# A hybrid attention, Fourier and Hyena layer on one core: merge gates and branch products computed token-major, their sum transposed on TensorE, and the adaLN gate summed and broadcast by one all-ones matrix

## The chip, the cores and the metric

One core of a Trainium2 chip runs the kernel. The metric is the device time of one execution in microseconds. The kernel before took 1326.72 us, the median of three runs (1324.34 to 1326.83). PE is the matrix engine TensorE, PEld its weight loads, DVE the vector engine, ACT the scalar engine, POOL GpSimd, and SP the engine that issues most DMAs here.

## The reference

One layer over 128 context and 256 latent tokens of 2048 channels, all in fp32. Cut to what this change touches:

```
proj, gate = _modulated_proj(y, c_ctx, norm_g, w_ada, b_ada, w_in)   # gate = last third of silu(c) @ w_ada + b_ada
y_a = att * silu(...)      # 1024 channels: neighbourhood attention, 8 heads
y_b = fourier * silu(...)  # 512 channels
y_c = hyena * silu(...)    # 512 channels
g_a, g_b, g_c = split(sigmoid(proj[..., OFF_MG:]), 3)      # 3 x 2048 channels
merged = g_a * (y_a @ w_br[:1024]) + g_b * (y_b @ w_br[1024:1536]) + g_c * (y_c @ w_br[1536:])
return x + gate[:, None, :] * (merged @ w_out)
```

The adaLN gate has one row of 2048 numbers for the context tokens and one for the latent tokens.

## The kernel before

**Products with the weights.** PE multiplies in fp32r. Each operand is split into a hi part (a cast) and a lo part (the rest), and a product is hi x hi + lo x hi + hi x lo: three matmuls. `products` (line 478) walks over pairs of k tiles: for each it loads a weight tile `w` of 2 x 128 rows and 512 columns (512 KB), lets ACT cast it to `wh` (line 473) and DVE subtract to `wl` (line 475), and issues first all matmuls with `wh`, then those with `wl`. There are 4 buffers of `w`, 2 of `wh`, 2 of `wl`, 5 PSUM banks `acc` for sums and 3 banks `aux` for everything else.

**Two layouts.** `chan_block` (line 504) makes a product channel-major, [channel, token]: the weights are the stationary side, 128 columns at a time, and 384 tokens stream; a pair of k tiles is 4 sums x 2 k tiles x 3 = 24 matmuls of 384 columns. `tok_block` (line 511) makes it token-major, [token, channel]: 128 tokens are stationary and 512 columns of the weights stream; a pair is 3 x 2 x 3 = 18 matmuls of 512 columns. The stationary side has the contracted channels on the partitions, so what enters a product (`h`, the branch outputs `y`, the merged sum `m`) must lie channel-major.

**The stages.** `main` (line 971) runs the Hyena input, then the Fourier and attention inputs, then, from line 987 on, the merge: for each of four blocks of 512 columns and each branch, a gate product of 8 pairs (sigmoid by ACT, line 994) and a branch product of 2, 2 or 4 pairs; DVE multiplies both (lines 999 and 1002) and POOL adds up (line 1003). The sum `merged` is channel-major. At the end it is split into `m` (line 1006). The output projection (line 1010) is token-major; DVE multiplies by the gate and adds x.

**The adaLN gate.** `ada_gate` (line 901) runs beside the merge stage. For each of four column blocks DVE multiplies 16 tiles of `w_ada` with the condition and adds them up into `part` (line 931), once for each of two rows; two fp32 matmuls by a matrix of ones with 32 columns (line 937) sum over the partitions into 32 rows, the bias is added, and at the end all is split. In the output stage `bcast_row` (line 294) picks one row and broadcasts it to 128 partitions by two fp32r matmuls for each row, four for each column block.

**The order.** `Weave` (line 130) writes the order of PE and SP in the program by a plan: each flow yields steps with a tensor time, a latency and events, and flows of lower number go first. The gate's flow is paced by 2.7 k tiles of the main flow for each of its 64 tiles (line 923). The order of ACT, DVE and POOL comes from the scheduler of the framework, by priority.

Of the kernel before, what the change touches and what calls it, by code (L numbers as in the profile page):

```python
# [10 lines left out]
F32 = mybir.dt.float32  # L11
# [7 lines left out]
P = 128  # L19
D = 2048  # L20
# [27 lines left out]
# (stream index, first token column, number of tokens, first 128-token tile, tiles)  # L48
# [6 lines left out]
def shape_constants():  # L55
    """Arrays that depend on the shapes alone."""
# [48 lines left out]
# blocks of adaLN columns: first column, columns, pace; and the sums of the Hyena input: block, pairs of k tiles  # L105
# [7 lines left out]
def small_arrays(a, consts):  # L113
    """Small arrays side by side: vectors with 128 channels on the partitions, one column each, and the identity;
    the positional features with the first two filter layers."""
    rows = [a["c"], a["c_ctx"], a["norm_g"], a["b_ada"][:, :2 * D], a["conv_w"], a["conv_b"], a["hy_bias"]]
    rows = np.concatenate([np.asarray(r).reshape(-1, P) for r in rows])
    half = np.concatenate([np.asarray(a[k]) for k in ("f_b1", "f_freq", "f_b2")])
    half = np.concatenate([half, half], axis=1)
    mlp = np.zeros((64, TOK + 192), np.float32)  # L120
    mlp[:33, :TOK] = consts.pop("zfeat")
    mlp[:33, TOK:TOK + 64] = np.asarray(a["f_w1"])[0]
    mlp[:, TOK + 64:] = np.concatenate([np.asarray(a["f_w2"])[0]] * 2, axis=1)
    a["f_w3"] = np.concatenate([np.asarray(a["f_w3"])[0]] * 2)
    a["mlp"] = mlp
    a["first"] = np.concatenate([np.concatenate([rows, half]).T, consts.pop("ident")], axis=1)
    a.update(consts)


class Weave:  # L130
    """Orders the steps of several flows for the in-order queues of TensorE and of the weight loads.

    A flow is a generator. Before each step it yields what the step asks for: the tensor time it holds, the time
    of its load, the latency after the flow's previous step, and events that come first. A flow of lower number
    goes first when its step is ready; the others fill in.
    """
# [77 lines left out]
def hybrid_block(ctx: ExitStack, tc: tile.TileContext, a: dict):  # L214
# [79 lines left out]
    def bcast_row(out, row, hi, lo):  # L294
        """One row of hi + lo to all partitions."""
        pick = ident_r[:, row:row + 1].broadcast_to([P, P])
        mm(out, pick, hi, True, False)
        mm(out, pick, lo, False, True)
# [28 lines left out]
    def rsqrt(out, ss, n, scale):  # L327
        """out = 1 / sqrt(ss * scale + EPS), all [P, n]."""
# [33 lines left out]
    def x_norm():  # L362
        """x channel-major as it comes, and 1 / rms of its tokens on all partitions."""
# [33 lines left out]
    def ada(b, c0, wd, pace, rate):  # L397
        """Columns c0 .. c0 + wd - 1 of shift and scale; then that part of h, hi and lo."""
# [66 lines left out]
    ahead = []  # L465

    def weights(src, kp, c0):
        """hi and lo parts of two k tiles of 512 columns, in two steps."""
# [9 lines left out]
    def products(src, c0, kps, n, product, evac, done=lambda kp: (), final=False):  # L478
        """n sums of the products of hi and lo parts, of two k tiles at a time: the ones with wh first, as wl comes
        later. A final block ends sum by sum, so that the evacuations spread out."""  # L480
# [23 lines left out]
    def chan_block(src, c0, kps, x, evac, done=lambda kp: ()):  # L504
        """Columns c0..c0+511, channel-major [channel, token]."""
# [4 lines left out]
    def tok_block(src, c0, x, evac, final=False):  # L510
        """Columns c0..c0+511, token-major [token, channel]."""
        def product(ps, t, kt, px, w, start, stop):
            mm(ps, x[px][kt // 4][:, kt % 4, P * t:P * t + P], w, start, stop)
        yield from products(src, c0, range(KT // 2), NT, product, evac, final=final)

# [1 line left out]
    # Even and odd tokens apart: E and O hold (real, imaginary, real with the top bin's row) of the filter's even and  # L517
    # odd part over bins 0..127; the top bin sits in row 0 of the imaginary products. C is the context's filter.
# [3 lines left out]
    def sin_layer(ps, n, col, name):  # L522
        """n rows of sin(freq * (ps + bias))."""
# [13 lines left out]
    def filters():  # L537
# [5 lines left out]
        def split_w3(x):  # L543
            """hi part on partitions 0..63, lo part on the others."""
# [110 lines left out]
    def long_conv(pool, o, z, xg):  # L655
        """z <- xg * (conv(z, filter o) + bias * z), channel-major, in place."""
# [53 lines left out]
    def fourier(u, gate):  # L710
        """Real part of the 2-D DFT of u, times the gate path (in place), channel-major."""
# [62 lines left out]
    def flip(x):  # L774
        """Latent tokens with the columns of each grid row in reverse."""
# [90 lines left out]
    # ================= the program =================  # L866
# [31 lines left out]
    # adaLN gate: rows 32 j hold columns 512 j .. 512 j + 511  # L898
    gate_rows = []

    def ada_gate():
# [4 lines left out]
        gate_b = pool.tile([P, 512], F32, name="gate_b")  # L906
        for j in range(4):
            nc.gpsimd.dma_start(out=gate_b[32 * j:32 * j + 32, :],
                                in_=b_ada[0, 2 * D + 512 * j:2 * D + 512 * j + 512].partition_broadcast(32))
        grow = [pool.tile([P, 512], F32, name=f"grow{s}") for s in range(2)]  # L910

        def load(i):
            w = pool.tile([P, 512], F32, tag="w_gate", name="w_gate", bufs=6)
# [5 lines left out]
        for j in range(4):  # L919
            part = [pool.tile([P, 512], F32, tag=f"part{s}", name=f"gate_part{s}", bufs=1) for s in range(2)]  # L920
            for kt in range(KT):
# [4 lines left out]
                for s in range(2):  # L926
                    cs = cond[:, kt, s:s + 1]
                    if kt == 0:
                        nc.vector.tensor_scalar(out=part[s], in0=w, scalar1=cs, scalar2=None, op0=ALU.mult)
                    else:  # L930
                        nc.vector.scalar_tensor_tensor(out=part[s], in0=w, scalar=cs, in1=part[s],  # L931
                                                       op0=ALU.mult, op1=ALU.add)
            yield step(0.5, lat=5.0)
            rows = slice(32 * j, 32 * j + 32)
            for s in range(2):
                pg = aux()
                mm(pg[rows, :], ones, part[s])
                nc.vector.tensor_tensor(out=grow[s][rows, :], in0=pg[rows, :], in1=gate_b[rows, :], op=ALU.add)
        for s in range(2):
            gate_rows.append(split(grow[s], pool.tile([P, 512], F32R, name=f"grow_hi{s}"),  # L940
                                   pool.tile([P, 512], F32R, name=f"grow_lo{s}")))
# [29 lines left out]
    def main():  # L971
# [15 lines left out]
        merged = []  # L987
        for ob in range(4):
            m32 = s6([P, 4, TOK], F32, f"merged{ob}")
            for bi, (br, kps) in enumerate(((2, (6, 7)), (1, (4, 5)), (0, (0, 1, 2, 3)))):  # L990
                g = s6([P, 4, TOK], F32, "mgate")

                def ev_gate(j, ps):
                    nc.scalar.activation(g[:, j, :], ps, AF.Sigmoid)
                yield from chan_block(w_in, OFF_MG + D * br + 512 * ob, range(8), h, ev_gate)

                def ev_br(j, ps):
                    if bi == 0:
                        nc.vector.tensor_tensor(out=m32[:, j, :], in0=ps, in1=g[:, j, :], op=ALU.mult)
                    else:  # L1000
                        t = tmp("mt")
                        nc.vector.tensor_tensor(out=t[:, 0:TOK], in0=ps, in1=g[:, j, :], op=ALU.mult)
                        nc.gpsimd.tensor_tensor(out=m32[:, j, :], in0=m32[:, j, :], in1=t[:, 0:TOK], op=ALU.add)  # L1003
                yield from chan_block(w_br, 512 * ob, kps, y, ev_br, lambda kp: (Y_READY[kp // 2],))
            merged.append(m32)
        m = list(zip(*[split_big(merged[ob], f"m{ob}") for ob in range(4)]))

# [1 line left out]
        osrc = [a["y_prompt"][0], a["y_sample"][0, 0:P, :], a["y_sample"][0, P:2 * P, :]]  # L1009
        for ob in range(4):  # L1010
            cs = slice(512 * ob, 512 * ob + 512)
            gts = []
            for s in range(2):
                yield step(MM2, after=("gate",), wait=4.0)
                pg = aux()
                bcast_row(pg, 32 * ob, *gate_rows[s])
                gt = s6([P, 512], F32, "gt")
                nc.scalar.copy(out=gt, in_=pg)
                gts.append(gt)

            def ev_out(t, ps):
# [3 lines left out]
                nc.vector.tensor_tensor(out=o, in0=ps, in1=gts[CONTEXT if t == 0 else LATENT], op=ALU.mult)  # L1025
# [3 lines left out]
            yield from tok_block(w_out, 512 * ob, m, ev_out, final=(ob == 3))  # L1029
# [42 lines left out]
```

## Time and profile before

| | us |
|---|---|
| median of three runs | 1326.72 |
| span of the profiled execution, all that the page gives of its time | 1331.5 |
| PE busy | 1296.1 (97%) |
| weight loads busy | 1172.4 (88%) |
| DVE busy | 712.7 (54%) |
| ACT busy | 456.6 (34%) |
| POOL busy | 191.4 (14%) |
| merge stage, from the first sigmoid to the end of the last branch product | 669.5 to about 1190 |
| output stage, its matmuls | 1190.9 to about 1324.5 |

The span is the time from the first to the last instruction in one execution. Matmuls follow each other before their results are out, so one is shown as busy for longer than the time to the next one's start; what counts on PE is the time from start to start. A line number is that of a helper where one is called: all matmuls stand at line 253, so the tiles tell them apart.

### The profile page before, as it was taken

What the parts mean: (1) busy time and instruction counts of PE and PEld (TensorE: products, weight loads), DVE (VectorE), ACT (ScalarE), POOL (GpSimd) and SP (SyncE); (2) the same over time, 40 slices, a digit from 0 to 9 for tenths busy, and PEclk for the clock granted to TensorE, in tenths of its full rate; (3) what the DMA queues carried; (4) which work ended last, traced back from release to release, by engine and by line L of the source; (5) the groups of instructions that cost most, each with busy time, mean ns of one, the idle gap of its engine ahead of it and who ended that gap; (6) DMA issues with size and microseconds to landing.
All of it is one profiled execution on the core that took longest, in us unless ns stands there. A gap on an engine that the chain in (4) does not pass through costs nothing.

```text
span 1331.5 us, 18263 instructions
## 1 busy us (share of the span) xinstructions
PE 1296.1 (97%) x7290; PEld 1172.4 (88%) x7290; DVE 712.7 (54%) x1076; ACT 456.6 (34%) x715; POOL 191.4 (14%) x211
## 2 busy tenths in 40 slices
PE   6889999999999999999999999999999999999997
PEld 4667879878888988889999999999999999998886
DVE  6567638868444335552354763754746733354442
ACT  4523324421343244433444222222222222242221
POOL 2046200135010002200110110011001100120000
PEclk9889999999999999999999999999999999999999
DMA  8888874322374446554453655554655544445551
GB/s 271 260 298 283 264 248 122 111 78 82 103 162 132 143 119 123 118 134 127 108 109 115 211 175 156 174 175 134 193 182 164 174 134 124 126 131 183 172 173 57
DMA packets 111189, 211.30 MB, mean 159 GB/s; under 512 B 8128, under 2 KB 16704, under 8 KB 111104
## 3 DMA queue, kind: packets, MB, share of 16 engines
q1 hardware_dynamic: 107200, 198.98, 48.0%
q0 software_dynamic: 3760, 11.01, 5.0%
q8 instruction: 57, 0.93, 0.3%
q14 instruction: 28, 0.23, 0.0%
q10 hardware_dynamic: 144, 0.14, 0.0%
HBM read 205.91 MB, written 4.19 MB: 158 GB/s over the span
## 4 chain that ended last, share of the span: by engine, by line
PE 91%; DMA 4%; DVE 2%; ACT 1%; POOL 1%; issue 0%; SPq 0%; ACTq 0%
PE acc L253 83%; PE aux L253 6%; DMA w<-in_w_in 3%; DVE wl L475 1%; DMA w_ada<-in_w_ada 1%; DMA x<-in_x_prompt 1%; ACT wh L473 1%; PE aux L851 0%; PE aux L783 0%; POOL yim L678 0%; DVE hc L634 0%; PE acc L376 0%; PE aux L663 0%; POOL yre L678 0%; DVE h_lo L455 0%
## 5 line engine op out<-in xcount | busy, mean ns | idle before, releaser
L475 DVE TENSOR_TENSOR wl<-w,wh 128x1024 fp32r<-128x1024 f32 x272 | 351.1, 1291 | 445.9 <-PE acc L253 308.7
L473 ACT CAST wh<-w 128x1024 fp32r<-128x1024 f32 x272 | 286.3, 1053 | 720.8 <-PE acc L253 635.5
L253 PE MATMUL acc<-h_hi,wh 128*128 128x384 f32 x1216 | 414.7, 341 | 7.7 <-DVE hc L634 2.8
L253 PE MATMUL acc<-h_lo,wh 128*128 128x384 f32 x1216 | 408.9, 336 | 0.0
L253 PEld LDWEIGHTS acc<-h_hi,wh 128*128 128x128 f32 x1216 | 230.0, 189 | 20.8 <-issue 11.1
L253 PE MATMUL acc<-h_hi,wl 128*128 128x384 f32 x1216 | 241.6, 337 | 0.0
L253 PEld LDWEIGHTS acc<-h_lo,wh 128*128 128x128 f32 x1216 | 230.0, 189 | 2.1 <-issue 0.7
L253 PEld LDWEIGHTS acc<-h_hi,wl 128*128 128x128 f32 x1216 | 212.2, 188 | 5.1 <-issue 4.4
L253 PE MATMUL acc<-wh,h_hi 128*128 128x512 f32 x336 | 135.6, 404 | 0.0
L253 PE MATMUL acc<-wh,h_lo 128*128 128x512 f32 x336 | 131.8, 392 | 0.0
L1003 POOL TENSOR_TENSOR merged<-merged,mt 128x384 f32<-128x384 f32 x32 | 40.7, 1302 | 426.8 <-ACT wh L473 240.6
L931 DVE SCALAR_TENSOR_TENSOR gate_part<-w_gate,cond,gate_part 128x512 f32<-128x512 f32 x120 | 88.0, 784 | 25.5 <-DMA w_gate<-in_w_ada 25.5
L253 PE MATMUL acc<-wl,h_hi 128*128 128x512 f32 x336 | 90.9, 400 | 0.0
L253 PEld LDWEIGHTS acc<-wh,h_hi 128*128 128x128 f32 x336 | 63.4, 189 | 13.2 <-issue 0.7
L253 PEld LDWEIGHTS acc<-wh,h_lo 128*128 128x128 f32 x336 | 63.4, 189 | 13.0 <-issue 0.7
L253 PE MATMUL acc<-wh,m_hi 128*128 128x512 f32 x192 | 74.7, 389 | 0.0
L253 PE MATMUL acc<-wh,m_lo 128*128 128x512 f32 x192 | 74.7, 389 | 0.0
L253 PEld LDWEIGHTS acc<-wl,h_hi 128*128 128x128 f32 x336 | 61.4, 188 | 12.9 <-issue 1.4
L253 PE MATMUL acc<-wl,m_hi 128*128 128x512 f32 x192 | 49.5, 389 | 0.0
L253 PE MATMUL acc<-ya_hi,wh 128*128 128x384 f32 x128 | 42.8, 334 | 0.0
L253 PE MATMUL acc<-ya_lo,wh 128*128 128x384 f32 x128 | 42.8, 334 | 0.0
L253 PEld LDWEIGHTS acc<-wh,m_lo 128*128 128x128 f32 x192 | 36.0, 188 | 7.5
(255 smaller groups left out, 1320.5 us busy)
## 6 DMA issues: line engine op xcount, KB each, us to landing
w<-in_w_in SPq DMA_DIRECT2D x208, 512.0 KB, 3.7
w_ada<-in_w_ada SPq DMA_DIRECT2D x48, 512.0 KB, 5.6
w<-in_w_br SPq DMA_DIRECT2D x32, 512.0 KB, 4.0
w_gate<-in_w_ada SPq DMA_DIRECT2D x64, 256.0 KB, 4.1
w<-in_w_out SPq DMA_DIRECT2D x32, 512.0 KB, 3.9
w_ada<-in_w_ada SPq DMA_DIRECT2D x32, 256.0 KB, 5.7
x<-in_x_sample SPq DMA_DIRECT2D x4, 512.0 KB, 12.6
bm<-in_rpb POOLq DMA_DIRECT2D x32, 64.0 KB, 5.8
```

The costliest lines, as they stand in the source:

```text
L253: nc.tensor.matmul(out, lhsT, rhs, start=start, stop=stop)
L473: nc.scalar.copy(out=wh, in_=w)
L475: nc.vector.tensor_tensor(out=wl, in0=w, in1=wh.bitcast(F32), op=ALU.subtract)
L931: nc.vector.scalar_tensor_tensor(out=part[s], in0=w, scalar=cs, in1=part[s], op0=ALU.mult, op1=ALU.add)
L1003: nc.gpsimd.tensor_tensor(out=m32[:, j, :], in0=m32[:, j, :], in1=t[:, 0:TOK], op=ALU.add)
```

## The change

The three gate products and three branch products of each block become token-major (`tok_block` in place of `chan_block`); `merged` then is [token, channel]. A new flow `merged_T` transposes it on PE, three 128x128 tiles for each group of 128 channels, and splits the PSUM bank straight into `m`: blocks 0 to 2 from the start of the last branch product on, block 3 after it, while the output projection's first pairs run. The output projection's steps wait by events for `m2` and the gate, and from the seventh pair on for `m3`. In the last branch product DVE adds in place of POOL.

The gate's bias row lies in row 0 of a zeroed tile and enters the first product's sum; each `part` is split, and two fp32r matmuls by a 128x128 matrix of ones sum over the partitions and give the sum to all 128 rows at once; ACT copies it to SBUF. `bcast_row` is no longer called in the output stage. The pool of the gate's weight tiles has 4 buffers where it had 6.

```
     def ada_gate():
...
-        gate_b = pool.tile([P, 512], F32, name="gate_b")
...
-        grow = [pool.tile([P, 512], F32, name=f"grow{s}") for s in range(2)]
+        bias = pool.tile([P, 512], F32, name="gate_bias")
+        nc.gpsimd.memset(bias, 0.0)
+        ones_r = pool.tile([P, P], F32R, name="ones_r")
+        nc.scalar.activation(ones_r, ident, AF.Copy, bias=1.0, scale=0.0)
+        for s in range(2):
+            gates.append(pool.tile([P, 4, 512], F32, name=f"gate{s}"))
...
-            w = pool.tile([P, 512], F32, tag="w_gate", name="w_gate", bufs=6)
+            w = pool.tile([P, 512], F32, tag="w_gate", name="w_gate", bufs=4)
...
         for j in range(4):
+            nc.gpsimd.dma_start(out=bias[0:1, :], in_=b_ada[0:1, 2 * D + 512 * j:2 * D + 512 * j + 512])
...
+                    before = bias if kt == 0 else part[s]
+                    nc.vector.scalar_tensor_tensor(out=part[s], in0=w, scalar=cond[:, kt, s:s + 1], in1=before,
+                                                   op0=ALU.mult, op1=ALU.add)
+            hl_ = [split(part[s], tmp("gate_hi", None, F32R), tmp("gate_lo", None, F32R)) for s in range(2)]
             for s in range(2):
+                yield step(MM2, lat=7.0 if s == 0 else 0.3)
                 pg = aux()
-                mm(pg[rows, :], ones, part[s])
-                nc.vector.tensor_tensor(out=grow[s][rows, :], in0=pg[rows, :], in1=gate_b[rows, :], op=ALU.add)
...
+                mm(pg, ones_r, hl_[s][0], True, False)
+                mm(pg, ones_r, hl_[s][1], False, True)
+                nc.scalar.copy(out=gates[s][:, j, :], in_=pg)
...
+        def merged_T(obs, lat):
+            for ob in obs:
+                m[0][ob], m[1][ob] = [s6([P, 4, TOK], F32R, f"m{ob}_{n}") for n in ("hi", "lo")]
+                for c in range(4):
+                    yield step(NT * TR, lat=lat)
+                    lat = 0.4
+                    pt = aux()
+                    for t in range(NT):
+                        nc.tensor.transpose(out=pt[:, P * t:P * t + P], in_=merged[ob][:, t, P * c:P * c + P],
+                                            identity=ident)
+                    split(pt[:, 0:TOK], m[0][ob][:, c, :], m[1][ob][:, c, :])
+            W.signal(f"m{obs[-1]}")
...
-                yield from chan_block(w_in, OFF_MG + D * br + 512 * ob, range(8), h, ev_gate)
+                yield from tok_block(w_in, OFF_MG + D * br + 512 * ob, h, ev_gate)
+                if ob == 3 and bi == 2:
+                    W.spawn(1, merged_T((0, 1, 2), 2.0))
...
+                        (nc.vector if ob == 3 and bi == 2 else nc.gpsimd).tensor_tensor(
+                            out=m32[:, t, :], in0=m32[:, t, :], in1=x, op=ALU.add)
+                yield from tok_block(w_br, 512 * ob, y, ev_br, kps=kps, done=lambda kp: (Y_READY[kp // 2],))
+        W.spawn(1, merged_T((3,), 4.0))
...
-            for s in range(2):
-                yield step(MM2, after=("gate",), wait=4.0)
-                pg = aux()
-                bcast_row(pg, 32 * ob, *gate_rows[s])
...
+            def done(kp):
+                return ("m2", "gate") if kp < 6 else ("m3",)
+            yield from tok_block(w_out, 512 * ob, m, ev_out, final=(ob == 3), done=done)
```

PE's row at the end of the last branch product and the start of the output projection, before. `grow_hi` and `grow_lo` are the split rows of the gate, `ident_r` picks one, `m` is the split sum.

```order
L253 MATMUL acc<-ya_hi,wh 128x384
L253 MATMUL acc<-ya_lo,wh 128x384
L253 MATMUL acc<-ya_hi,wl 128x384 x8
L253 MATMUL aux<-grow_hi_9516,ident_r 128x512
L253 MATMUL aux<-grow_lo_9517,ident_r 128x512
L253 MATMUL aux<-grow_hi_9520,ident_r 128x512
L253 MATMUL aux<-grow_lo_9521,ident_r 128x512
L253 MATMUL acc<-wh,m_hi 128x512
L253 MATMUL acc<-wh,m_lo 128x512
```

PE's row inside the last branch product after the change. `first` holds the identity, `merged` is the sum that is transposed.

```order
L253 MATMUL acc<-wh,ya_hi 128x512
L253 MATMUL acc<-wh,ya_lo 128x512
L996 MATMUL aux<-first,merged_5411 128x128 x3
L253 MATMUL acc<-wl,ya_hi 128x512 x2
L996 MATMUL aux<-first,merged_5411 128x128 x3
L253 MATMUL acc<-wl,ya_hi 128x512 x2
L996 MATMUL aux<-first,merged_5411 128x128 x3
L253 MATMUL acc<-wl,ya_hi 128x512 x2
L996 MATMUL aux<-first,merged_5411 128x128 x3
L253 MATMUL acc<-wh,ya_hi 128x512
L253 MATMUL acc<-wh,ya_lo 128x512
```

The broadcasts are gone from the start of the output projection, and groups of three transposes stand between the matmuls of the branch product, a group behind every second or fourth matmul, twelve of them; four more stand in the second pair of the output projection.

DVE's row from the first transposed block to the last one, after the change. `wl` are the lo parts of the weights for the pairs to come, `m_lo` reads a transposed bank.

```order
L302 TENSOR_TENSOR m_lo<-aux,m_hi 128x384 x2
L475 TENSOR_TENSOR wl<-w,wh 128x1024
L302 TENSOR_TENSOR m_lo<-aux,m_hi 128x384 x6
L475 TENSOR_TENSOR wl<-w,wh 128x1024
L302 TENSOR_TENSOR m_lo<-aux,m_hi 128x384 x4
L475 TENSOR_TENSOR wl<-w,wh 128x1024
L1017 TENSOR_TENSOR mt<-acc,mgate 128x512 x3
L1018 TENSOR_TENSOR merged_8476<-merged_8476,mt 128x512 x3
L475 TENSOR_TENSOR wl<-w,wh 128x1024 x2
L302 TENSOR_TENSOR m_lo<-aux,m_hi 128x384 x4
```

Before, DVE had four `m_lo` of 128x1536 there, which read `merged` in SBUF; now it has sixteen of 128x384, which read PSUM banks, with a `wl` between them.

PE's row around one sum of the adaLN gate, before: `gate_part` are the products that DVE added up, `ones` has 32 columns.

```order
L253 MATMUL acc<-h_lo,wh 128x384
L253 MATMUL acc<-h_hi,wl 128x384 x4
L253 MATMUL aux<-gate_part_8761,ones 32x512
L253 MATMUL aux<-gate_part_8762,ones 32x512
L253 MATMUL acc<-h_hi,wl 128x384 x4
```

The same place after the change.

```order
L253 MATMUL acc<-wh,h_lo 128x512
L253 MATMUL aux<-gate_hi,ones_r 128x512
L253 MATMUL aux<-gate_lo,ones_r 128x512
L253 MATMUL acc<-wh,h_hi 128x512
L253 MATMUL acc<-wh,h_lo 128x512
L253 MATMUL acc<-wh,h_hi 128x512
L253 MATMUL acc<-wh,h_lo 128x512
L253 MATMUL aux<-gate_hi,ones_r 128x512
L253 MATMUL aux<-gate_lo,ones_r 128x512
L253 MATMUL acc<-wl,h_hi 128x512 x6
```

Two fp32 matmuls, each of them two instructions of PE in the trace, have become four fp32r ones in two steps.

## Rows read from the trace of the kernel before

**Rows 1.** The page: engines busy, and the chain that ended last by engine.

```profile
PE 1296.1 (97%) x7290; PEld 1172.4 (88%) x7290; DVE 712.7 (54%) x1076; ACT 456.6 (34%) x715; POOL 191.4 (14%) x211
...
PE 91%; DMA 4%; DVE 2%; ACT 1%; POOL 1%; issue 0%; SPq 0%; ACTq 0%
```

**Rows 2.** PE's waits from 620 us on: who waited for whom, us, times, longest.

```profile
PE acc L253 <- ACT gateA L743: 0.9, 1, 0.9
PE aux L253 <- ACT pcT L856: 0.8, 1, 0.8
```

**Rows 3.** Timeline of ACT, merge stage: start, us, what [idle before].

```profile
862.31 1.05 ACT L473 CAST wh<-w 128x1024 fp32r<-128x1024 f32 x1 [1.58 <-PE acc L253]
...
878.95 1.05 ACT L473 CAST wh<-w 128x1024 fp32r<-128x1024 f32 x1 [3.10 <-PE acc L253]
```

**Rows 4.** Timeline of ACT, output stage.

```profile
1298.68 1.05 ACT L473 CAST wh<-w 128x1024 fp32r<-128x1024 f32 x1 [3.02 <-PE acc L253]
...
1315.00 1.05 ACT L473 CAST wh<-w 128x1024 fp32r<-128x1024 f32 x1 [3.02 <-PE acc L253]
```

**Rows 5.** Windows, merge and output stage: us, engines busy, clock, DMA.

```profile
1112.00:1188.00 76.00, 76.00 (x440) 76.00 (x440) 31.43 (x28) 26.01 (x29) 4.92 (x4) 1.00 0.41 125
1228.00:1256.00 28.00, 28.00 (x125) 23.21 (x124) 8.58 (x7) 6.85 (x7) 2.13 (x4) 1.00 0.57 180
```

**Rows 6.** Timeline of PE in a token-major product of w_in.

```profile
503.03 0.39 PE L253 MATMUL acc<-wh,h_hi 128*128 128x512 f32 x1
...
507.11 0.39 PE L253 MATMUL acc<-wh,h_hi 128*128 128x512 f32 x1
```

**Rows 7.** Chain of waits from 820 us on: start, us, what.

```profile
832.50 1.83 PE aux L253 x4
834.34 90.34 PE acc L253 x520
...
1108.37 1.83 PE aux L253 x4
...
1223.78 0.92 PE aux L253 x4
1224.70 32.65 PE acc L253 x144
```

**Rows 8.** DVE's instructions from 740 us on: busy, mean ns, idle before.

```profile
L475 DVE TENSOR_TENSOR wl<-w,wh 128x1024 fp32r<-128x1024 f32 x138 | 174.7, 1266 | 222.7 <-PE acc L253 159.3 <-ACT wh L473 41.8 <-ACT mgate L994 20.9
L931 DVE SCALAR_TENSOR_TENSOR gate_part<-w_gate,cond,gate_part 128x512 f32<-128x512 f32 x115 | 83.1, 772 | 25.5 <-DMA w_gate<-in_w_ada 25.5
L1002 DVE TENSOR_TENSOR mt<-acc,mgate 128x384 f32<-128x384 f32 x28 | 13.7, 550 | 9.6 <-PE acc L253 9.5
L1025 DVE TENSOR_TENSOR o<-acc,gt 128x512 f32<-128x512 f32 x12 | 7.7, 686 | 11.2 <-PE acc L253 11.2
```

**Rows 9.** ACT's instructions from 740 us on.

```profile
L473 ACT CAST wh<-w 128x1024 fp32r<-128x1024 f32 x137 | 144.3, 1054 | 400.4 <-PE acc L253 400.4
L994 ACT ACTIVATE mgate<-acc 128x384 f32<-128x384 f32 x40 | 16.2, 490 | 0.0
...
L1018 ACT COPY gt<-aux 128x512 f32<-128x512 f32 x8 | 4.3, 588 | 2.3 <-PE aux L253 2.3
```

**Rows 10.** Timeline of PE around two groups of transposes.

```profile
570.86 0.49 PE L851 MATMUL aux<-first,st 128*128 128x128 f32 x3
571.10 1.63 PE L253 MATMUL acc<-wl,h_hi 128*128 128x512 f32 x6
572.57 0.49 PE L851 MATMUL aux<-first,st 128*128 128x128 f32 x3
572.81 0.48 PE L253 MATMUL acc<-wh,h_hi 128*128 128x512 f32 x1
```

**Rows 11.** SP's waits: us in total, times, longest.

```profile
SPq L470 <- DVE wl L475: 868.7, 230, 12.2
```

**Rows 12.** DMA issues by line: count, KB each, median us to landing.

```profile
w<-in_w_in SPq DMA_DIRECT2D x208, 512.0 KB, 3.7
```

More of the change, by code (lines that the diff above doesn't have):

```diff
@@ L508, in chan_block, with tok_block @@
         yield from products(src, c0, kps, 4, product, lambda j, ps: evac(j, ps[:, 0:TOK]), done)
-    def tok_block(src, c0, x, evac, final=False):
+    def tok_block(src, c0, x, evac, final=False, kps=range(KT // 2), done=lambda kp: ()):
         def product(ps, t, kt, px, w, start, stop):
             mm(ps, x[px][kt // 4][:, kt % 4, P * t:P * t + P], w, start, stop)
-        yield from products(src, c0, range(KT // 2), NT, product, evac, final=final)
+        yield from products(src, c0, kps, NT, product, evac, done, final=final)
     specE, specO, specC = [None] * 2, [None] * 2, [None] * 2
@@ L896, in fnet @@
         W.signal("yb")
-    gate_rows = []
+    gates = []
     def ada_gate():
@@ L905, in ada_gate @@
         base = W.steps + 2
-        gate_b = pool.tile([P, 512], F32, name="gate_b")
-        for j in range(4):
-            nc.gpsimd.dma_start(out=gate_b[32 * j:32 * j + 32, :],
-                                in_=b_ada[0, 2 * D + 512 * j:2 * D + 512 * j + 512].partition_broadcast(32))
-        grow = [pool.tile([P, 512], F32, name=f"grow{s}") for s in range(2)]
+        bias = pool.tile([P, 512], F32, name="gate_bias")
[4 more added lines that the diff above has]
+            gates.append(pool.tile([P, 4, 512], F32, name=f"gate{s}"))
         def load(i):
-            w = pool.tile([P, 512], F32, tag="w_gate", name="w_gate", bufs=6)
+            w = pool.tile([P, 512], F32, tag="w_gate", name="w_gate", bufs=4)
             kt, c = i % KT, 2 * D + 512 * (i // KT)
@@ L926, in ada_gate @@
                 for s in range(2):
[L927 to L934, printed above, removed]
+                    before = bias if kt == 0 else part[s]
+                    nc.vector.scalar_tensor_tensor(out=part[s], in0=w, scalar=cond[:, kt, s:s + 1], in1=before,
+                                                   op0=ALU.mult, op1=ALU.add)
+            hl_ = [split(part[s], tmp("gate_hi", None, F32R), tmp("gate_lo", None, F32R)) for s in range(2)]
             for s in range(2):
+                yield step(MM2, lat=7.0 if s == 0 else 0.3)
                 pg = aux()
-                mm(pg[rows, :], ones, part[s])
-                nc.vector.tensor_tensor(out=grow[s][rows, :], in0=pg[rows, :], in1=gate_b[rows, :], op=ALU.add)
-        for s in range(2):
-            gate_rows.append(split(grow[s], pool.tile([P, 512], F32R, name=f"grow_hi{s}"),
-                                   pool.tile([P, 512], F32R, name=f"grow_lo{s}")))
+                mm(pg, ones_r, hl_[s][0], True, False)
+                mm(pg, ones_r, hl_[s][1], False, True)
+                nc.scalar.copy(out=gates[s][:, j, :], in_=pg)
         W.signal("gate")
@@ L984, in main @@
             yield from qkv(hf)
-        merged = []
+        merged, m = [None] * 4, ([None] * 4, [None] * 4)
+        def merged_T(obs, lat):
[10 more added lines that the diff above has]
+            W.signal(f"m{obs[-1]}")
@@ L988, in main, with ev_gate, ev_br @@
         for ob in range(4):
-            m32 = s6([P, 4, TOK], F32, f"merged{ob}")
+            m32 = merged[ob] = s6([P, NT, 512], F32, f"merged{ob}")
             for bi, (br, kps) in enumerate(((2, (6, 7)), (1, (4, 5)), (0, (0, 1, 2, 3)))):
-                g = s6([P, 4, TOK], F32, "mgate")
-                def ev_gate(j, ps):
-                    nc.scalar.activation(g[:, j, :], ps, AF.Sigmoid)
-                yield from chan_block(w_in, OFF_MG + D * br + 512 * ob, range(8), h, ev_gate)
-                def ev_br(j, ps):
+                g = s6([P, NT, 512], F32, "mgate")
+                def ev_gate(t, ps):
+                    nc.scalar.activation(g[:, t, :], ps, AF.Sigmoid)
+                yield from tok_block(w_in, OFF_MG + D * br + 512 * ob, h, ev_gate)
+                if ob == 3 and bi == 2:
+                    W.spawn(1, merged_T((0, 1, 2), 2.0))
+                def ev_br(t, ps):
@@ L998, in ev_br @@
                     if bi == 0:
-                        nc.vector.tensor_tensor(out=m32[:, j, :], in0=ps, in1=g[:, j, :], op=ALU.mult)
+                        nc.vector.tensor_tensor(out=m32[:, t, :], in0=ps, in1=g[:, t, :], op=ALU.mult)
                     else:
-                        t = tmp("mt")
-                        nc.vector.tensor_tensor(out=t[:, 0:TOK], in0=ps, in1=g[:, j, :], op=ALU.mult)
-                        nc.gpsimd.tensor_tensor(out=m32[:, j, :], in0=m32[:, j, :], in1=t[:, 0:TOK], op=ALU.add)
@@ L1004, in main @@
-                yield from chan_block(w_br, 512 * ob, kps, y, ev_br, lambda kp: (Y_READY[kp // 2],))
-            merged.append(m32)
-        m = list(zip(*[split_big(merged[ob], f"m{ob}") for ob in range(4)]))
+                        x = tmp("mt")
+                        nc.vector.tensor_tensor(out=x, in0=ps, in1=g[:, t, :], op=ALU.mult)
+                        (nc.vector if ob == 3 and bi == 2 else nc.gpsimd).tensor_tensor(
+                            out=m32[:, t, :], in0=m32[:, t, :], in1=x, op=ALU.add)
@@ L1011, in main @@
             cs = slice(512 * ob, 512 * ob + 512)
-            gts = []
-            for s in range(2):
-                yield step(MM2, after=("gate",), wait=4.0)
-                pg = aux()
-                bcast_row(pg, 32 * ob, *gate_rows[s])
-                gt = s6([P, 512], F32, "gt")
-                nc.scalar.copy(out=gt, in_=pg)
-                gts.append(gt)
             def ev_out(t, ps):
@@ L1024, in ev_out @@
                 o = tmp("o")
-                nc.vector.tensor_tensor(out=o, in0=ps, in1=gts[CONTEXT if t == 0 else LATENT], op=ALU.mult)
+                nc.vector.tensor_tensor(out=o, in0=ps, in1=gates[CONTEXT if t == 0 else LATENT][:, ob, :], op=ALU.mult)
                 last = ob == 3
@@ L1028, in ev_out @@
                 (nc.sync if last else nc.gpsimd).dma_start(out=osrc[t][:, cs], in_=o)
-            yield from tok_block(w_out, 512 * ob, m, ev_out, final=(ob == 3))
+            def done(kp):
+                return ("m2", "gate") if kp < 6 else ("m3",)
+            yield from tok_block(w_out, 512 * ob, m, ev_out, final=(ob == 3), done=done)
     x_loads()
```

## The prediction

> **What bounds the kernel now.** I read the page first, then the chain of waits, then what PE waited for, then the timelines of PE and ACT inside the stage that the change rewrites. On the page PE is busy for 97% of the span, and the chain that ended last lies on PE for 91% [rows 1]. From 620 us to the end PE waited twice, 1.7 us together [rows 2]. So in the merge stage and in the output stage there is nothing to hide behind: a matmul taken out of PE's row shortens the kernel by its own start-to-start time, and one put in lengthens it, as long as the weights and the PSUM banks keep coming. The reader is to see the rate in two places. ACT casts the weights of one pair of k tiles after the other, and each cast waits for PE. In the merge stage, with 24 matmuls of 384 columns to a pair, four casts further is 878.95 - 862.31 = 16.64 us, so 4.16 us a pair [rows 3]. In the output stage, with 18 matmuls of 512 columns to a pair, it is 1315.00 - 1298.68 = 16.32 us, so 4.08 us [rows 4]. Both pairs stream 9216 columns, and both stretches run at a granted clock of 1.00, the 2.4 GHz level [rows 5].
>
> **The change part by part.**
>
> *Merge gates and branch products token-major.* Four column blocks, each with three gate products of 8 pairs and branch products of 2, 2 and 4 pairs, are 4 x 32 = 128 pairs. 3072 matmuls of 384 columns go, 2304 of 512 columns come. Each pair goes from 4.16 to 4.08 us, if h and y as the stationary side run as m does in the output stage. That they do is seen in a product of w_in that is token-major already: a pair begins at 503.03 us and the next at 507.11, which is 4.08 again [rows 6]. The sum is 128 x 0.08 = 10.2 us less. The chain gives the upper end: 90.34 / 520 = 0.1737 us and 32.65 / 144 = 0.2267 us for one matmul, so 24 x 0.1737 - 18 x 0.2267 = 0.088 us a pair, 11.3 us [rows 7]. I take 10.2, since the chain's longer pieces also carry the joints around the gate sums, which I count next.
>
> The rows put it like this: 4.16 / 24 = 173.3 ns is 13.3 ns over 384 / 2.4, and 4.08 / 18 = 226.7 ns is 13.3 ns over 512 / 2.4. About 13 ns belong to the matmul and not to its columns, and 6 x 128 = 768 matmuls less save them. The Trainium skill (TensorE: Matmul & The Clock Gate, section Back-to-back issue gap) puts the gap between isolated matmuls at N / 2.4 plus 2.5 ns, and says that in a stream with weight loads both set the spacing. By its 2.5 ns 768 matmuls less would be worth an estimated 1.9 us. The trace does not agree: it has 13.3 ns at both widths.
>
> *The gate's sums.* Before, each of the four column blocks has two fp32 matmuls by the 32 columns of ones, 4 PE instructions, which hold the chain for 1.83 us [rows 7]. From one such place to the fourth it is (1108.37 - 832.50) / 3 = 91.96 us, and the pace of 2.7 k tiles a step puts 16 x 2.7 / 2 = 21.6 pairs between them, 89.86 us at 4.16. The rest, 2.10 us, is what one place costs with its joints. Four are 8.4 us (7.3 by 1.83). They go. The sums of after are 16 fp32r matmuls of 512 columns, and the broadcasts of before, which go too, were 16 of the same form, 0.92 us for four [rows 7]. These cancel: they move from the output stage to the merge stage.
>
> *Their inputs.* ACT and DVE gain eight splits and eight PSUM copies of 128x512, 0.59 (ACT) and 0.69 us (DVE) each by the nearest rows [rows 8, 9], and lose the sums with the bias row and the copies of the broadcast. By the order each fp32r sum stands over two pairs behind the split that it needs, so I cost its wait at nothing; if PE came first it would stand for a split, about 1.3 us, four times. The first product of a block now adds the bias row; it becomes a DVE instruction of the 0.77 us kind [rows 8], beside PE.
>
> *Transposes.* 16 groups of three 128x128 fp32 transposes come. The trace has that form between the same kind of matmuls: a group starts at 570.86 and the next matmul at 571.10; the six from there reach to the start of the next group at 572.57, 1.47 us where 6 x 0.2267 is 1.36; and that group goes to 572.81 [rows 10]. That is 0.24 + 0.11 = 0.35 us a group, 5.6 us for 16. From below it is 0.24, 3.8 us; from above the whole 0.49 us that a group is shown as busy, 7.8 us. I take 5.6, which holds the joint.
>
> *Who must keep up with them.* A transposed bank is read by ACT and then by DVE before it is free; by the nearest rows, which read 128x384 out of PSUM, that is 0.49 and 0.55 us [rows 8, 9]. There are three such banks. The first 12 groups stand in about two and a half pairs, some 11 us of PE, and in them DVE has 12 x 0.55 + 3 x 1.27 = 10.4 us and ACT 12 x 0.49 + 2 x 1.05 = 8.0 us to do [rows 8, 9]. The tightest place is the fourth group, which needs the bank of the first. That bank is filled 0.27 us behind the group's start, then ACT casts a wh that stands ahead (1.05), then come 0.49 and 0.55: about 2.3 us. PE arrives there three groups and three pairs of matmuls later, 3 x (0.35 + 0.45) = 2.4 us. So I cost the wait at nothing, and know that it is tight. The last block's four groups stand 4.08 + 4 x 0.2267 = 5.0 us behind the end of the branch product, and DVE needs three products and three sums of 0.69 us from the first finished bank on, which end about 3.2 us behind it. No wait, with 1.8 us to spare. The sums of that block sit on DVE; the others stay on POOL, blocks ahead of their use. In before, the split of m was on no one's path either, so nothing is gained there.
>
> *Queues.* w_gate has 4 buffers where it had 6, so its load i + 3 waits for DVE's step i - 1 instead of i - 3, and behind it in SP's row stand the loads of w. SP's own wait in that row is for wl, 230 times [rows 11], and in the order only 5 of the 64 loads carry a wait for DVE of their own (7 before). The casts of all 137 pairs waited for PE and none for a DMA [rows 9]. I cost it at nothing; without that cover it is the third rival. The bias rows are four small DMAs of POOL instead of four larger ones.
>
> Sum: -10.2 - 8.4 + 5.6 = -13.0 us. The page gives the profiled execution as its span alone, 1331.5 us, so 1318.5 us there. The median of the runs is 1326.72, 4.8 below that span; taken off it, 1313.7 us. The bounds give -11.3 - 8.4 + 3.8 = -15.9 and -10.2 - 7.3 + 7.8 = -9.7, so 1310.8 to 1317.0; the three runs lie 2.5 us apart, so the forecast's own range is 1309.5 to 1317.5.
>
> **The rivals.**
>
> *The transposes stall PE.* DVE's row has a wl (1.27 us) between the groups' m_lo three times. If DVE is late by one of them at three places, and the last block loses 1 us, 3 x 1.27 + 1, that is some 4.8 us: 1318.5. For it: DVE and ACT are nearly full in that stretch. Against: three banks, and the round through ACT and DVE is 1.04 us of work.
>
> *The rate stays.* If the 13 ns went with the columns and not with the matmuls, the first term would be 0 and the time 1326.7 - 8.4 + 5.6 = 1323.9. With the 2.5 ns of the Trainium skill it would be an estimated 1322.0. Against: rows 4 and 6 show the new form at 4.08.
>
> *Slower: the loads of w starve.* SP is in order. If DVE's step on w_gate comes late, the load of w behind it is late, the cast is late, and then wl and the next step. A w lands 3.7 us after its issue [rows 12]. With four buffers it goes out once wl of the fourth pair before is done, about three pairs or 12.5 us ahead of its own cast, so over 8 us pass before the cast feels it. It decides from there on: at 0.5 us for each of 64 loads, 32 us, the time is 1326.7 - 13.0 + 32 = 1345.7; it beats the gain from 0.20 us a load. For it: DVE waited 25.5 us for w_gate before, with 6 buffers [rows 8]. Against: none of that reached PE.
>
> **How the numbers follow.** The forecast 0.69, the stalls 0.20, the rate 0.05, the starved loads 0.04, and 0.02 for a time below the forecast's range. What a measurement of this kernel can tell from no change is about 0.2%, 2.7 us, so 1324.1 and above is not faster. Forecast and stalls are faster, the rate mostly (0.03 of 0.05), the starved loads slower: faster 0.93, same 0.03, slower 0.04; I shade these to 0.91, 0.05 and 0.04 for what I have not seen. The range reaches from below the forecast's own to past the stalls: 1308.5 to 1320.
>
> **What would show it.** In the merge stage of the new profile casts of wh should stand 4.08 us apart; matmuls of acc should be 5232 instead of 6000 at 384 and 512 columns; each gate sum should hold the chain for 0.45 us twice; PE should have no wait on m_lo or merged in the last block. The step on the rate is wrong if pairs of the merge stage stand at 4.16; the one on transposes is wrong if PE waits for DVE m_lo or if a group costs over 0.49 us; the one on queues is wrong if PE or the cast waits for w or w_gate. A time above 1320 would make the prediction wrong.

## The result: 1313.45 us, 1.0% faster, and the profile after

The changed kernel took 1313.45 us, the median of four runs (1310.38 to 1316.43), against 1326.78 for the kernel before on the same chips. The ratio of the runs is 0.9898, 95% interval 0.9872 to 0.9925. The forecast was 1313.7.

The span of the profiled execution fell from 1331.5 to 1313.7 us, which is 17.8 and not 13 us. A mark that both kernels pass shows why. The first sigmoid of `gateB`, whose code and all code ahead of it are the same, began at 338.9 us before and at 334.3 us after. This row of the kernel before, and the one of after, give operation, count, durations, and first and last start:

```profile
L743 ACT ACTIVATE gateB<-acc x4: 482/488/502, 338.9 to 340.1; 128x384 f32<-128x384 f32 x4
```

```profile
L743 ACT ACTIVATE gateB<-acc x4: 482/488/502, 334.3 to 335.4; 128x384 f32<-128x384 f32 x4
```

So 4.6 us of the difference belong to the start of the kernel in that one execution. From the mark to the end of the span it is 1331.5 - 338.9 = 992.6 us before and 1313.7 - 334.3 = 979.4 after: 13.2 us less. This stretch is the measure in all that follows; in nine executions the mark itself lay anywhere from 330.3 to 338.9 us, which is more than most effects that were to be told apart. How well the measure repeats is seen in the code that all nine kernels share behind the mark: up to the last sigmoid of `gateA` it took 291.7 or 291.8 us in every one of them.

The page of after, engines and the chain by engine, to be held against [rows 1]:

```profile
PE 1281.3 (98%) x6554; PEld 1072.6 (82%) x6554; DVE 716.1 (55%) x1077; ACT 461.7 (35%) x722; POOL 186.3 (14%) x201
...
PE 94%; DMA 3%; DVE 1%; ACT 1%; POOL 1%; issue 0%; SPq 0%; ACTq 0%
```

PE is as full as it was, with 736 fewer instructions in its row: 768 matmuls and 16 broadcasts less, 48 transposes more. Its only wait from 620 us on, which answers to [rows 2]:

```profile
PE acc L253 <- ACT gateA L743: 0.6, 1, 0.6
```

The timeline of ACT in the merge stage, which answers to [rows 3]:

```profile
856.20 1.06 ACT L473 CAST wh<-w 128x1024 fp32r<-128x1024 f32 x1 [3.03 <-PE acc L253]
...
872.52 1.06 ACT L473 CAST wh<-w 128x1024 fp32r<-128x1024 f32 x1 [3.02 <-PE acc L253]
```

From the first of these casts to the fourth behind it 16.32 us pass, 4.08 from cast to cast, where it was 16.64. The chain of waits around the second gate sum and in the last branch product, which answers to [rows 7] and shows the transposes (L996):

```profile
834.85 86.61 PE acc L253 x382
921.45 0.47 PE aux L253 x2
921.92 0.46 PE acc L253 x2
922.38 0.46 PE aux L253 x2
922.84 88.42 PE acc L253 x390
...
1157.23 0.47 PE acc L253 x2
1157.70 0.33 PE aux L996 x3
1158.03 0.47 PE acc L253 x2
```

A gate sum holds the chain for 0.93 us where the two fp32 matmuls held it for 1.83, the broadcasts of the output stage are gone, and a group of transposes holds it for 0.33 us.

### The profile page after: what moved, and what is told of

Its sections match the earlier page's. It is cut to its first block, busy times and chain, and to the rows that moved or that the text cites. A ratio compares the mean times of both kernels' runs of the same rounds, so it can differ in the third digit from the quotient of the medians.

```text
span 1313.7 us, 16781 instructions
## 1 busy us (share of the span) xinstructions
PE 1281.3 (98%) x6554; PEld 1072.6 (82%) x6554; DVE 716.1 (55%) x1077; ACT 461.7 (35%) x722; POOL 186.3 (14%) x201
## 4 chain that ended last, share of the span: by engine, by line
PE 94%; DMA 3%; DVE 1%; ACT 1%; POOL 1%; issue 0%; SPq 0%; ACTq 0%
PE acc L253 86%; PE aux L253 6%; DMA w<-in_w_in 1%; DMA w_ada<-in_w_ada 1%; DMA x<-in_x_prompt 1%; PE aux L851 0%; PE aux L783 0%; PE aux L996 0%; POOL yim L678 0%; DVE wl L475 0%; PE acc L376 0%; ACT wh L473 0%; PE aux L663 0%; POOL yre L678 0%; DVE f_n L529 0%
## 5 line engine op out<-in xcount | busy, mean ns | idle before, releaser
L253 PE MATMUL acc<-wh,h_hi 128*128 128x512 f32 x912 | 361.0, 396 | 0.6 <-ACT gateA L743 0.6
L253 PE MATMUL acc<-wh,h_lo 128*128 128x512 f32 x912 | 356.1, 390 | 0.0
L253 PE MATMUL acc<-wl,h_hi 128*128 128x512 f32 x912 | 239.9, 395 | 0.0
L253 PEld LDWEIGHTS acc<-wh,h_lo 128*128 128x128 f32 x912 | 171.5, 188 | 35.0 <-issue 0.7
L253 PE MATMUL acc<-h_hi,wh 128*128 128x384 f32 x448 | 155.2, 347 | 5.7 <-DVE hc L634 2.0
L253 PE MATMUL acc<-h_lo,wh 128*128 128x384 f32 x448 | 151.6, 338 | 0.0
L253 PEld LDWEIGHTS acc<-h_hi,wh 128*128 128x128 f32 x448 | 85.1, 190 | 16.6 <-issue 7.8
L253 PE MATMUL acc<-h_hi,wl 128*128 128x384 f32 x448 | 90.2, 339 | 0.0
L253 PEld LDWEIGHTS acc<-h_lo,wh 128*128 128x128 f32 x448 | 85.1, 190 | 2.2 <-issue 0.7
L253 PEld LDWEIGHTS acc<-h_hi,wl 128*128 128x128 f32 x448 | 78.4, 188 | 3.4 <-issue 2.7
```

The source lines that it names most:

```text
L253: nc.tensor.matmul(out, lhsT, rhs, start=start, stop=stop)
```

## The experiments

PE is taken to be the bound: what enters or leaves its row counts with its own time, and other engines count only where PE waits for them. Each kernel was profiled once and timed beside the kernel before. The stretches:

| kernel | time, us | ratio to before, 95% interval | span - first sigmoid | stretch |
|---|---|---|---|---|
| before | 1326.78 | | 1331.5 - 338.9 | 992.6 |
| changed | 1313.45 | 0.9898 (0.9872 to 0.9925) | 1313.7 - 334.3 | 979.4 |
| gate alone | 1318.19 | 0.9927 (0.9901 to 0.9953) | 1317.9 - 333.4 | 984.5 |
| merge alone | 1321.70 | 0.9954 (0.9941 to 0.9968) | 1318.0 - 330.3 | 987.7 |
| transposes twice | 1319.55 | 0.9943 (0.9918 to 0.9968) | 1316.4 - 331.7 | 984.7 |
| halves of 256 columns | 1341.35 | 1.0099 (1.0065 to 1.0133) | 1339.0 - 331.0 | 1008.0 |
| 3 buffers of w_gate | 1315.73 | 0.9919 (0.9895 to 0.9944) | 1314.3 - 335.0 | 979.3 |
| transposes in a row | 1315.76 | 0.9923 (0.9895 to 0.9950) | 1317.6 - 335.3 | 982.3 |
| last block early | 1315.80 | 0.9923 (0.9902 to 0.9945) | 1317.9 - 334.0 | 983.9 |

The medians of the last three kernels lie within 0.1 us of each other and can't tell them apart. That two of them are slower than the changed kernel by their stretches, 2.9 and 4.5 us, rests on one profile each and on the waits that it shows.

### The gate alone

The changed kernel with the merge stage of before.

```
-                yield from tok_block(w_in, OFF_MG + D * br + 512 * ob, h, ev_gate)
...
+                yield from chan_block(w_in, OFF_MG + D * br + 512 * ob, range(8), h, ev_gate)
...
-        W.spawn(1, merged_T((3,), 4.0))
...
+        m = list(zip(*[split_big(merged[ob], f"m{ob}") for ob in range(4)]))
```

> The new adaLN gate alone; the merge gates and branch products are channel-major as before, and the sum is split as before. Stretches are taken from the first sigmoid of gateB to the end of the span, since the start of the kernel is the same code and moved by itself: before 1331.5 - 338.9 = 992.6 us, after 1313.7 - 334.3 = 979.4. Theory (what leaves PE's row counts in full): the four fp32 sums go, 8.4 us, and the broadcasts only move, so 984.2 and about 1318 us. Rival (all of the gain is the rate of the pairs): 992.6 and 1326.8 us.

Measured: 984.5, 8.1 us less than before. The rival is out. Its chain of waits around the first gate sum, with 384-column matmuls around it:

```profile
829.07 0.46 PE aux L253 x2
829.53 0.70 PE acc L253 x4
830.23 0.46 PE aux L253 x2
830.69 89.45 PE acc L253 x516
```

### The merge alone

The changed kernel with the gate of before: fp32 sums and broadcasts in the output stage.

```
...
+            gts = []
+            for s in range(2):
+                yield step(MM2, after=("gate",), wait=4.0)
+                pg = aux()
+                bcast_row(pg, 32 * ob, *gate_rows[s])
...
```

> Token-major merge with the transposes, and the adaLN gate of before. Same stretch, 992.6 us before. Theory (13.3 ns for each matmul saved, 768 of them, and 16 groups of transposes at 0.33 to 0.35 us): -10.2 + 5.4, so 987.8 and about 1322 us. Rival (a matmul saved is worth 2.5 ns, the rest of the gain is the gate's): -1.9 + 5.4, so 996.1 and about 1330 us, slower than before.

Measured: 987.7, 4.9 us less than before, and faster by the runs too. A kernel whose saved matmuls were worth 2.5 ns each would have been slower than before. The two halves add up: 8.1 + 4.9 = 13.0 against 13.2 for both.

### Transposes twice

```
-                    for t in range(NT):
+                    for t in 2 * tuple(range(NT)):
                         nc.tensor.transpose(out=pt[:, P * t:P * t + P], in_=merged[ob][:, t, P * c:P * c + P],
```

> The changed kernel with every group's three transposes issued twice into the same bank, so 48 transposes more and no new joint and no more work for ACT and DVE. Same stretch, 979.4 us in the changed kernel. Theory (a transpose costs its start-to-start time of 0.08 us on PE): 16 x 0.24 = 3.9 us more, 983.3. Rival (the transposes stand in time that PE would have waited for weights or banks): 979.4. Rival (a group costs what it is shown busy, 0.49 us): 7.8 us more, 987.2.

Measured: 984.7, 5.3 us more than the changed kernel. All three expectations missed. The transposes are not hidden, which was the main question; but 48 more of them cost as much as the chain gives the first 48, 16 x 0.33 us, not less. The chain of this kernel, a group of six:

```profile
1154.31 0.66 PE aux L996 x6
1154.97 0.46 PE acc L253 x2
1155.43 0.66 PE aux L996 x6
```

It is 0.66 us where a group of three was 0.33, so a transpose costs 0.11 us and there is no joint. The 0.24 us that the timeline shows from a group's start to the next matmul's is too short, and the 0.1 us by which the matmuls behind it come late belong to the transposes.

### Halves of 256 columns

```
-            mm(ps, x[px][kt // 4][:, kt % 4, P * t:P * t + P], w, start, stop)
+            for c in range(0, 512, 512 // n):
+                mm(ps[:, c:c + 512 // n], x[px][kt // 4][:, kt % 4, P * t:P * t + P], w[:, c:c + 512 // n],
+                   start and c == 0, stop and c == 512 - 512 // n)
```

with n = 2 in the merge gates and branch products, n = 1 elsewhere.

> The changed kernel with each 512-column matmul of the merge gates and branch products cut into two of 256 columns, so 36 matmuls to a pair instead of 18, same columns. Same stretch, 979.4 us in the changed kernel. Theory (13.3 ns belong to each matmul): 256 / 2.4 + 13.3 = 120 ns, 36 x 0.120 = 4.32 us a pair, 0.24 more, 128 pairs: 30.7 us more, 1010. Rival (the short form was bound by its weight loads, one in 173 ns as in the pairs of before): 36 x 0.1733 = 6.24 us a pair, 276 us more, 1255. Rival (2.5 ns for a matmul): 18 x 128 x 2.5 ns = 5.8 us more, 985.

Measured: 1008.0, 28.6 us more than the changed kernel; both rivals are far off. Two pieces of its chain:

```profile
841.04 91.66 PE acc L253 x764
...
934.09 93.59 PE acc L253 x780
```

91.66 / 764 = 0.1200 us for a matmul of 256 columns. With 0.1733 at 384 and 0.2267 at 512 that is 13.3 ns over the columns at 2.4 GHz for each of three widths. Each half has a weight load of its own in the trace, so matmuls and loads were doubled together. By the chain's times, 0.1200 and 0.2267, the sum would be 30.5 us, 1.9 more than measured. Some 1.5 of them lie ahead of the first gate sum, where the attention's steps stand between the pairs; why is open.

### Three buffers of w_gate

```
-            w = pool.tile([P, 512], F32, tag="w_gate", name="w_gate", bufs=4)
+            w = pool.tile([P, 512], F32, tag="w_gate", name="w_gate", bufs=3)
```

and N_AHEAD 2 instead of 3.

> The changed kernel with 3 buffers of w_gate and its loads 2 steps ahead, where it had 4 and 3. Stretch from the first sigmoid of gateB to the end, 979.4 us in the changed kernel. Theory (the loads of w have over 8 us of cover, and PE does not feel SP's row): 979.4, while DVE waits longer for w_gate than the 43.3 us of the changed kernel. Rival (the third of the prediction: the row of SP starves the loads of w): 0.2 to 0.5 us for each of 64 loads, 992 to 1011.

Measured: 979.3, no difference. DVE's wait for w_gate in the changed kernel, and then in this one (us in total, times, longest):

```profile
DVE gate_part L931 <- DMA w_gate<-in_w_ada: 43.3, 39, 2.9
```

```profile
DVE gate_part L931 <- DMA w_gate<-in_w_ada: 50.8, 44, 4.1
```

The wait doubles from the 25.5 us of [rows 8] to 50.8 over both steps, and none of it reaches PE. The rival itself is hardly strained by this kernel: its load i + 2 waits for DVE's step i - 1, as load i + 3 did in the changed kernel, so only the time from a load to its use got shorter. What bears on the rival is SP's own wait for that step, in the kernel before, the changed one and this one:

```profile
SPq L915 <- DVE gate_part L929: 24.7, 3, 9.2
```

```profile
SPq L917 <- DVE gate_part L931: 17.8, 4, 10.6
```

```profile
SPq L917 <- DVE gate_part L931: 19.1, 5, 10.5
```

SP stood there only 1.3 us longer than in the changed kernel.

### Transposes in a row

```
-                    yield step(NT * TR, lat=lat)
+                    if len(obs) == 1 or (ob, c) == (0, 0):
+                        yield step(NT * TR, lat=lat)
```

> The changed kernel with the first 12 groups of transposes in one piece, 36 in a row, instead of between the matmuls of the last branch product. Same stretch, 979.4 us in the changed kernel. Theory (a bank comes free only after ACT's 0.49 and DVE's 0.55 us, and three banks don't cover a row): PE's own 36 x 0.11 = 4.0 us become about 0.3 + 0.5 + 9 x 0.56 + 0.8 = 6.6 us, so 2.6 us more, 982.0, and PE waits for DVE m_lo. Rival (only PE's own time counts): 979.4 and no such wait.

Measured: 982.3, 2.9 us more than the changed kernel, and PE waits for the banks. Its timeline of PE:

```profile
1157.69 1.15 PE L997 MATMUL aux<-first,merged 128*128 128x128 f32 x9
1159.96 1.48 PE L997 MATMUL aux<-first,merged 128*128 128x128 f32 x9 [1.12 <-DVE m_lo L302]
1161.67 3.31 PE L997 MATMUL aux<-first,merged 128*128 128x128 f32 x18 [0.23 <-DVE m_lo L302]
1164.74 1.62 PE L253 MATMUL acc<-wl,ya_hi 128*128 128x512 f32 x6
```

Three groups fill the three banks, then PE goes at the pace of ACT and DVE: 7.05 us for what takes 4.0 between matmuls. This is the stall that the first rival feared; the order of the changed kernel avoids it. The granted clock stayed at 1.00 in it (windows as in the next experiment):

```profile
1157.70:1164.70 7.00, 5.52 (x36) 3.65 (x35) 4.87 (x10) 5.67 (x12) 1.07 (x2) 1.00 0.42 138
```

### The last block early

```
-        W.spawn(1, merged_T((3,), 4.0))
+        W.spawn(1, merged_T((3,), 0.0))
```

> The changed kernel with the last block's transposes planned right behind the last branch product instead of 4 us later. Same stretch, 979.4 us in the changed kernel. Theory (the four groups are free of waits in the changed kernel only since a pair of the output projection stands ahead of them): DVE ends its three products and three sums 3.0 us behind the last matmul of the branch product (1177.48 against 1174.51 in the changed kernel), and PE stands for that, 982.4. Rival (the place does not matter, the sums are done in time): 979.4.

Measured: 983.9, 4.5 us more, where 3.0 were expected. Its timeline of PE:

```profile
1176.11 0.30 PE L996 MATMUL aux<-first,merged 128*128 128x128 f32 x1 [1.76 <-DVE merged L1018]
1176.62 0.33 PE L996 MATMUL aux<-first,merged 128*128 128x128 f32 x1 [0.21 <-DVE merged L1018]
1177.22 0.33 PE L996 MATMUL aux<-first,merged 128*128 128x128 f32 x1 [0.28 <-DVE merged L1018]
...
1177.88 0.63 PE L253 MATMUL acc<-wh,m_hi 128*128 128x512 f32 x1
1178.31 0.63 PE L253 MATMUL acc<-wh,m_lo 128*128 128x512 f32 x1
...
1181.40 0.48 PE L253 MATMUL acc<-wh,m_hi 128*128 128x512 f32 x1
```

The wait is there, for DVE's sums, 2.25 us of it shown as idle. Behind it the matmuls start 0.43 us apart instead of 0.23. The windows of the same kernel, ahead of the wait, in the slow stretch and behind it (us, busy time of PE, PEld, DVE, ACT and POOL, clock, DMA share, GB/s):

```profile
1170.00:1173.00 3.00, 3.00 (x15) 2.49 (x14) 1.23 (x1) 0.01 (x1) 0.00 (x0) 1.00 0.37 103
...
1177.80:1181.00 3.20, 3.20 (x10) 2.42 (x10) 1.52 (x3) 0.74 (x2) 0.00 (x0) 0.50 0.54 154
1181.00:1185.00 4.00, 4.00 (x21) 3.30 (x20) 1.49 (x3) 1.91 (x3) 0.00 (x0) 0.97 0.11 39
```

The granted clock was 0.50, the 1.2 GHz level, in that window of 3.2 us. That is where the other 1.5 us are: from 1177.88 to 1181.40 us, 3.5 us, six matmuls and two groups of transposes start, which take 6 x 0.2267 + 2 x 0.33 = 2.0 us elsewhere.

## Why the prediction was right

**The rate.** Costed at 10.2 us, from two rows 0.08 us apart. The merge alone gained 4.9 us, and its transposes cost 16 x 0.33 = 5.3, so the rate gave 10.2. The upper end of 11.3, from the chain, held joints as was said. The step rested on the reading that about 13 ns belong to each matmul; the halves confirm it with a width that no row of before had. The 2.5 ns of the Trainium skill (TensorE: Matmul & The Clock Gate, section Back-to-back issue gap) are, by that section, for an isolated matmul with no allowance for weight loads; here every matmul has its own load, and the trace has 13.3 ns at 256, 384 and 512 columns. For a stream of such pairs the same section gives about 131 ns at 512 columns; this trace has 226.7, and the measurement decides. Whether the weight load is what takes them was not tried. Some rows of the changed kernel bear on it, from a stretch with the granted clock at 1.00: matmuls of 512 columns with only 32 columns of weights. Their load is shown as 0.11 us where one of 128 columns is 0.19, and they still stand 0.23 us apart, so there the length of the load does not set it; whether a load as such does is open.

```profile
168.73 0.62 PE L253 MATMUL aux<-evod,fwd_hi 128*32 128x512 f32 x2
169.19 0.39 PE L253 MATMUL aux<-evod,fwd_lo 128*32 128x512 f32 x1
169.42 0.33 PE L253 MATMUL acc<-h_hi,wh 128*128 128x384 f32 x1
```

```profile
168.95 0.11 PEld L253 LDWEIGHTS aux<-evod,fwd_lo 128*32 128x32 f32 x1
169.19 0.19 PEld L253 LDWEIGHTS acc<-h_hi,wh 128*128 128x128 f32 x1
```

**The gate's sums.** Costed at 8.4 us with the broadcasts cancelling; measured 8.1 alone. The chain's 1.83 us for each place would have given 7.3, so the way through the distance from place to place was the better reading.

**The transposes.** Costed at 5.6 us, 5.3 measured. The sum was near and its parts were not: 0.24 for the group and 0.11 for a joint should have been three times 0.11.

**Who must keep up.** Costed at nothing, and called tight. The changed kernel's timeline of DVE at the first transposes:

```profile
1158.39 1.02 DVE L302 TENSOR_TENSOR m_lo<-aux,m_hi 128x384 fp32r<-128x384 f32 x2 [2.89 <-ACT m_hi L301]
1159.33 1.22 DVE L475 TENSOR_TENSOR wl<-w,wh 128x1024 fp32r<-128x1024 f32 x1
```

and of PE:

```profile
1156.74 0.49 PE L996 MATMUL aux<-first,merged 128*128 128x128 f32 x3
...
1159.13 0.49 PE L996 MATMUL aux<-first,merged 128*128 128x128 f32 x3
```

The first group starts at 1156.74 and its bank is free about half of 1.02 us behind 1158.39, so some 2.2 us later; the fourth group comes at 1159.13, 2.4 us later. The prediction had 2.3 and 2.4. For the last block, DVE's sums and the transposes that need them:

```profile
1175.60 1.88 DVE L1018 TENSOR_TENSOR merged<-merged,mt 128x512 f32<-128x512 f32 x3
```

```profile
1179.50 0.49 PE L996 MATMUL aux<-first,merged 128*128 128x128 f32 x3
```

DVE ends at 1177.48, 2.0 us ahead; 1.8 was foreseen. The two experiments that take this room away, the row and the early block, cost 2.9 and 4.5 us in their profiles, with waits of PE in both, so the cover was real and not merely unneeded.

**Queues.** Costed at nothing, and PE felt nothing. But the prediction had called this step wrong if a cast waits for w, and one cast did. ACT's waits from 730 us on in the changed kernel:

```profile
ACT wh L473 <- PE acc L253: 352.2, 127, 3.1
ACT wh L473 <- DVE wl L475: 15.1, 5, 3.0
...
ACT wh L473 <- DMA w<-in_w_in: 3.2, 1, 3.2
```

Once a cast did stand for a load, 3.2 us, and five times for a wl that DVE did late. None of it reached PE, whose only wait is the 0.6 us above. SP stood 17.8 us for DVE's steps on w_gate, in four places, against 24.7 before; so the third rival had no ground here.

**The chances.** The likeliest case came true in its mechanism and in its size; none of the rivals did. That the median hit the forecast within 0.3 us is in part luck: the four runs lie 6 us apart, and two parts of the transposes' sum erred against each other. What speaks for the working is the stretch, 13.2 us where 13.0 were forecast, and its two halves. By the prediction's own shares the chances add up to 0.94 for faster and 0.02 for the same, not 0.93 and 0.03; nothing hangs on it.

## What to carry to other kernels

When TensorE bounds a stage and runs in short matmuls, look at the start-to-start time at two widths that the trace already has: the part that is left over the columns was paid for each matmul here, and the layout with the fewer, wider matmuls is worth its transposes if these are few (here 48 transposes, 5.3 us, for 768 matmuls, 10.2 us). Put such transposes between matmuls that don't depend on them, so far apart that the banks come free, and far enough behind the engine that fills their source. Take small differences from a mark that both kernels pass to the end, not from whole spans.

## What the runs showed of the hardware that was not expected

- A short wait was followed by a slower clock and so cost more than its own length. In the kernel with the last block early, PE idled 1.76, 0.21 and 0.28 us around a few transposes, and behind them the granted clock was 0.50 in a window of 3.2 us, with 512-column matmuls 0.43 us apart; in the kernel with the transposes in a row, idle times of 1.12 and 0.23 us left the clock at 1.00. The Trainium skill (TensorE: Matmul & The Clock Gate, section HAM oscillation — how this bites in real kernels) has waits for DMA that leave TensorE without work lower the clock, time after time; this trace agrees in that the clock fell behind idle time, though the wait was for DVE. It is one execution, and what of it lowered the clock is not shown.
- A 128x128 fp32 transpose costs PE 0.11 us in a stream, 0.33 for three and 0.66 for six, though the rows show starts 0.08 us apart and a busy time of 0.49 us for three.
- The start of the kernel, the same code in all nine kernels, reached its first sigmoid of gateB between 330.3 and 338.9 us. The mean granted clock up to there was 0.97 to 0.99, with 0.99 in the shortest; what else differed is open.
